# Three matmul passes per product against two: activation halves laid side by side in a two-block float32 kernel on one core

## The chip, the cores and the metric

The kernel runs on one core of one Trainium2 chip. The metric is device time in microseconds (us), the median of three runs. The engines named below are PE (TensorE, the matrix engine), DVE (VectorE), ACT (ScalarE), POOL (GpSimd) and SP (SyncE, which issues the weight DMAs). PE multiplies a moving operand (up to 512 columns) by 128x128 stationary weights and writes PSUM, a memory of eight banks of 512 float32 columns by 128 partitions.

## The reference

Two transformer blocks stand one behind the other, for 256 tokens of 1024 features, all in float32:

```
x = x + 0.5 * swiglu(rms_norm(x), gate 1024x2816, up, down 2816x1024)      # FFN1
h = rms_norm(x);  z = h @ w_in + b_in                                      # mix
x = x + (sig(g0) * (window_attention(z) @ w_a) + sig(g1) * (mlstm(z) @ w_m)) @ w_out
x = rms_norm(x + 0.5 * swiglu(rms_norm(x), ...))                           # FFN2
h = rms_norm_2(x);  z = h @ w_in                                           # mix2
x = x + concat(gated_linear_attention(z), latent_attention(z)) @ w_out
x = x + cross_attention(rms_norm_2(x), mem) @ w_o                          # xa
f = rms_norm_2(x)                                                          # FFN3
return x + (silu(causal_conv(f @ gate)) * (f @ up)) @ down
```

The result has to agree with this at float32 accuracy, so a single pass of reduced precision over a product is not enough.

## The kernel before

Activations lie mostly as [feature, token]: a tile of 128 features by T = 256 tokens, eight tiles for the 1024 features of `x`. Weights are streamed: SP fetches chunks of up to 1 MB into one of three raw buffers (`wraw`), and `halves` splits them into a high half `wh` (an ACT copy that rounds to the matrix format, L339) and a low half `wl` (a DVE subtraction, L340), six buffers each. Activations are split in the same way, `xh` by ACT and `xl` by DVE (`x_done`, L449 and L450, which also apply the norm's gain).

A float32 product is the sum of three passes, xh·wh + xl·wh + xh·wl. Where the result is wanted as [feature, token], `mm3` (L361 to L363) issues three matmuls of 256 moving columns for each 128x128 block of weights, all into the same 256 columns of PSUM. Where the result is wanted as [token, feature], `mm3n` (L367 to L369) has the weights moving, 272 to 512 columns; the diff leaves its three passes as they are. `mm3` is called 2208 times: 1584 in the three FFNs (each 44 column blocks by 8 for gate and up, 8 by 22 for down), 464 in mix, 160 in mix2 and xa.

`lin_t` computes a chunk of 256 output columns: two blocks j of 256 tokens, side by side in one PSUM bank. The PSUM pool `mm` has four buffers of one bank; the pool `at` has the four other banks. When a chunk is done, `scaled` (L512, L514) multiplies it by the norm's factor r per token on DVE, and so takes it out of PSUM. In an FFN a pair is one chunk of the gate (`pg`) and one of up (`pu`): s = pg·r, silu of it on ACT, a = s·pu, and the split of a. In FFN3 the gate passes a convolution over three tokens first (L562 to L564).

The instruction order on each engine comes from the framework's scheduler, which orders instructions by priorities and by its own estimate of when they can run; each engine then works strictly in that order and waits for semaphores of the others. A tile can be written again only when its last reader is through, so the number of PSUM buffers sets how far PE can run ahead of DVE and ACT.

Of the kernel before, what the change touches and what calls it, by code (L numbers as in the profile page):

```python
# [111 lines left out]
def column_vectors():  # L112
    """(key, input, index) of vectors by feature, 128 to a column."""
# [35 lines left out]
def lay_out(I):  # L149
    """The inputs as they lie in DRAM: the same numbers in another order."""  # L150
# [37 lines left out]
class Builder:  # L188
    """Activations lie as [feature, token] ("T") or as [token, feature] ("N"). A float32 product
    x*w is carried by three float32r passes over exact halves: xh*wh + xl*wh + xh*wl."""  # L190

    def __init__(self, ctx, tc, I, out):
# [6 lines left out]
        self.mm = pool("mm", 4, space=PSUM)  # L199
# [15 lines left out]
    def phase(self, name):  # L215
        """A pool for the tiles of one phase, also for its temporaries."""
# [9 lines left out]
    def pm(self):  # L226
        return self.mm.tile([P, 512], F32, tag="mm", name=self.n("mm"))
# [5 lines left out]
    def load_x(self):  # L233
        """x and the first weights, in the order of the features."""
# [20 lines left out]
    def row(self, name, a, n, tag, bufs=2):  # L255
        """Part of a row vector, on all partitions."""
# [5 lines left out]
    def consts(self):  # L262
# [19 lines left out]
        # gains of the latent attention's parts that aren't rotated, and the dimension's root  # L282
# [3 lines left out]
        # for the sums of squares of x * gain  # L286
# [4 lines left out]
        # additive masks of the window: [previous block | current block],  # L291
        # and of the causal attention: [all | current block]
# [7 lines left out]
        # [key, query] mask, once for each diagonal block of the mLSTM  # L300
# [9 lines left out]
        # minus the identity, once for each half  # L310
# [3 lines left out]
        # ones where source <= target  # L314
# [6 lines left out]
    def wraw(self, key, a=0, n=None):  # L321
        """A chunk (or elements a..a+n of each partition) of the weights."""
# [8 lines left out]
    def halves(self, v):  # L331
        """hi, lo of a view [P, n], n <= 1024."""
# [10 lines left out]
    def wcols(self, key, nt, kt=KD, per=1, early=False):  # L343
        """Halves of a "t" chunk as nt pairs [P, kt, 128]; per tiles of 128 columns are split at once."""
# [26 lines left out]
    def lin_t(self, key, xh, xl, kt=KD, early=False):  # L371
# [8 lines left out]
    def lin_n(self, key, n, xh, xl, kt=KD, pool=None):  # L380
        """Two PSUM tiles [128 tokens, n] of x @ (the "n" chunks of n columns), n <= 512."""
        ps = [(pool or self.pm)() for _ in range(TB)]
        for k, kk, runs in n_runs(n, kt):
            raw = self.wraw(f"{key}.{k}")
            for s, m in runs:
                hi, lo = self.halves(raw[:, s * n:(s + m) * n])
                for i in range(m):
                    q = k + s + i
                    for b in range(TB):
                        self.mm3n(ps[b][:, :n], xh[q][:, b * P:b * P + P], xl[q][:, b * P:b * P + P],  # L390
# [3 lines left out]
    def xtiles(self, k):  # L394
        xh = self.xp.tile([P, T], F32R, tag=f"xh{k}", name=self.n(f"xh{k}"))
        xl = self.xp.tile([P, T], F32R, tag=f"xl{k}", name=self.n(f"xl{k}"))
        return xh, xl

    def lin_first(self, key, xh, xl, raw=None):
        """Two PSUM views [P, 256] of x @ (a "t" chunk of 256 columns), that wait as little for the last of x.  # L400
        With raw, a "q" chunk, x too is split part by part."""
        ps = [self.pa()[:, :T] for _ in range(2)]
        if raw is None:
            hv = self.wcols(key, 2)
            for ks in (range(6), range(6, 8)):
                for j in range(2):
                    for k in ks:
                        self.mm3(ps[j], hv[j][0][:, k, :], hv[j][1][:, k, :], xh[k], xl[k], k == 0, k == 7)
        else:
            for q in range(4):  # L410
                for d in (2 * q, 2 * q + 1):
                    self.x_done(d)
                    xh.append(self.halved[d][0])
                    xl.append(self.halved[d][1])
# [8 lines left out]
    def rsqrt(self, y, v, shape):  # L423
        """y = 1/sqrt(v), by a step of Newton's method and one of third order."""
# [3 lines left out]
        # 3/8 of y * (3 - v y^2) / 2, then y * (15 - 10 h + 3 h^2) / 8, h = v y^2  # L428
# [11 lines left out]
    def then(self, gcol, tiles=None):  # L440
        """The gain of the norm that follows, and where the halves of x * gain go."""
        self.gcol, self.gtiles, self.halved = gcol, tiles or self.xtiles, {}

    def x_done(self, d):
        """Halves of x[d] * gain, for the norm that follows."""
        nc = self.nc
        h, l = self.gtiles(d)
        g = self.gcol[:, d:d + 1]
        nc.scalar.activation(h, self.x[d], AF.Copy, scale=g)  # L449
        nc.vector.scalar_tensor_tensor(l, self.x[d], g, h.bitcast(F32), ALU.mult, ALU.subtract)  # L450
        self.halved[d] = h, l

    def split_x(self):
        return [[self.halved[d][i] for d in range(KD)] for i in range(2)]
# [17 lines left out]
    def mean(self, acc, tag):  # L472
        """The mean over features by token, [P, TB]."""
# [6 lines left out]
    def sums(self, ps, i, acc):  # L480
        """Sums over partitions of acc[:, :T], to columns 2i, 2i+1 of ps."""
# [3 lines left out]
    def rinv_n(self, mean, tag="rN"):  # L485
        """1/rms by token, and the mean square with its guard."""
# [7 lines left out]
    def by_token(self, rn, tag="rB"):  # L494
        """[P, TB] (token on partitions) to [P, T], the same on all partitions."""
# [11 lines left out]
    def scaled(self, out, ps, r):  # L507
        """out [P, 2, T] = ps * r, ps being one PSUM tile or two."""
        tt = self.nc.vector.tensor_tensor
        if isinstance(ps, list):  # L510
            for j in range(2):
                tt(out[:, j, :], ps[j], r, ALU.mult)  # L512
        else:
# [1042 lines left out]
```

## Time and profile before

| | |
|---|---|
| median of 3 runs | 1031.64 us (1031.37 to 1032.19) |
| the profiled execution | known by its span, 1030.0 us from the first to the last instruction |
| PE busy | 1012.6 us, 98% of the span |
| DVE busy | 687.3 us, 67% |
| ACT busy | 548.7 us, 53% |
| POOL busy | 68.0 us, 7% |
| mean granted TensorE clock | 0.998 of full speed |

The span lies 1.64 us under the median: what stands around it (launch, end) is not in the trace. Busy time of PE is a modelled pipelined time, so that the distance from one matmul's start to the next says more on its pace than the duration in a row. "Idle before" in a row is the time in which an engine stood still ahead of these instructions, with what released it.

### The profile page before, as it was taken

What the parts mean: (1) busy time and instruction counts of PE and PEld (TensorE: products, weight loads), DVE (VectorE), ACT (ScalarE), POOL (GpSimd) and SP (SyncE); (2) the same over time, 40 slices, a digit from 0 to 9 for tenths busy, and PEclk for the clock granted to TensorE, in tenths of its full rate; (3) what the DMA queues carried; (4) which work ended last, traced back from release to release, by engine and by line L of the source; (5) the groups of instructions that cost most, each with busy time, mean ns of one, the idle gap of its engine ahead of it and who ended that gap; (6) DMA issues with size and microseconds to landing.
All of it is one profiled execution on the core that took longest, in us unless ns stands there. A gap on an engine that the chain in (4) does not pass through costs nothing.

```text
span 1030.0 us, 18987 instructions
## 1 busy us (share of the span) xinstructions
PE 1012.6 (98%) x7770; PEld 964.4 (94%) x7770; DVE 687.3 (67%) x1212; ACT 548.7 (53%) x936; POOL 68.0 (7%) x200
## 2 busy tenths in 40 slices
PE   6999999999999999999999999999899999999998
PEld 6999999999866799999999999998789899999998
DVE  7756556557966657567655665678967778777642
ACT  5644444458745554545544544468855656655431
POOL 4200000010000010000100020012000401000000
PEclk9999999999999999999999999999999999999999
DMA  6755545545343325445554645446305425555560
GB/s 229 268 183 186 179 169 185 185 167 207 128 155 129 123 92 196 164 164 197 188 190 173 226 160 182 160 163 221 148 2 205 164 87 210 195 175 183 161 199 22
DMA packets 28520, 173.00 MB, mean 168 GB/s; under 512 B 3712, under 2 KB 5008, under 8 KB 10128
## 3 DMA queue, kind: packets, MB, share of 16 engines
q1 hardware_dynamic: 26640, 169.88, 46.7%
q10 hardware_dynamic: 1728, 1.88, 0.6%
q8 instruction: 61, 1.00, 0.4%
q14 instruction: 27, 0.22, 0.1%
q0 software_dynamic: 64, 0.02, 0.0%
HBM read 170.72 MB, written 1.05 MB: 167 GB/s over the span
## 4 chain that ended last, share of the span: by engine, by line
PE 93%; DVE 2%; DMA 2%; POOL 1%; issue 1%; ACT 0%; DVEq 0%; POOLq 0%; ACTq 0%
PE mm L362 24%; PE mm L363 24%; PE mm L361 24%; PE mm L367 3%; PE mm L368 3%; PE mm L369 3%; PE at L656 1%; PE at L692 1%; DMA wr<-in_wts 1%; PE at L363 1%; PE at L362 1%; PE at L361 1%; DVE wl L340 1%; PE at L687 1%; DMA posi<-in_pos 1%
## 5 line engine op out<-in xcount | busy, mean ns | idle before, releaser
L339 ACT ACTIVATE wh<-wr 128x1024 fp32r<-128x1024 f32 (+5 forms) x380 | 340.3, 913 | 375.2 <-PE mm L362 262.1
L340 DVE TENSOR_TENSOR wl<-wr,wh 128x1024 fp32r<-128x1024 f32 (+5 forms) x380 | 391.8, 1043 | 209.8 <-ACT wh L339 208.7
L363 PE MATMUL mm<-xh,wl 128*128 128x256 f32 x1296 | 367.2, 283 | 0.2 <-DVE wl L340 0.2
L362 PE MATMUL mm<-xl,wh 128*128 128x256 f32 x1296 | 367.3, 283 | 0.0
L361 PE MATMUL mm<-xh,wh 128*128 128x256 f32 x1296 | 367.2, 284 | 0.0
L363 PEld LDWEIGHTS mm<-xh,wl 128*128 128x128 f32 x1296 | 248.6, 192 | 0.7 <-DVE wl L340 0.4
L362 PEld LDWEIGHTS mm<-xl,wh 128*128 128x128 f32 x1296 | 248.6, 192 | 0.3 <-issue 0.3
L361 PEld LDWEIGHTS mm<-xh,wh 128*128 128x128 f32 x1296 | 248.5, 192 | 0.1
L361 PE MATMUL mm<-ah,wh 128*128 128x256 f32 x528 | 149.5, 283 | 0.0
L362 PE MATMUL mm<-al,wh 128*128 128x256 f32 x528 | 149.4, 283 | 0.0
L363 PE MATMUL mm<-ah,wl 128*128 128x256 f32 x528 | 149.4, 283 | 0.0
L362 PEld LDWEIGHTS mm<-al,wh 128*128 128x128 f32 x528 | 101.4, 192 | 0.0
L361 PEld LDWEIGHTS mm<-ah,wh 128*128 128x128 f32 x528 | 101.4, 192 | 0.0
L363 PEld LDWEIGHTS mm<-ah,wl 128*128 128x128 f32 x528 | 101.4, 192 | 0.0
L367 PE MATMUL mm<-wh,xh 128*128 128x512 f32 (+2 forms) x160 | 61.6, 386 | 0.0
L369 PE MATMUL mm<-wh,xl 128*128 128x512 f32 (+2 forms) x160 | 61.2, 382 | 0.0
L368 PE MATMUL mm<-wl,xh 128*128 128x512 f32 (+2 forms) x160 | 60.7, 380 | 0.0
L367 PEld LDWEIGHTS mm<-wh,xh 128*128 128x128 f32 x160 | 30.1, 188 | 7.1 <-issue 2.3
L363 PE MATMUL mm<-b16h,wl 128*128 128x256 f32 x128 | 36.3, 284 | 0.0
L362 PE MATMUL mm<-b16l,wh 128*128 128x256 f32 x128 | 36.2, 283 | 0.0
L361 PE MATMUL mm<-b16h,wh 128*128 128x256 f32 x128 | 36.2, 283 | 0.0
L368 PEld LDWEIGHTS mm<-wl,xh 128*128 128x128 f32 x160 | 30.1, 188 | 5.8 <-issue 1.1
(510 smaller groups left out, 1341.9 us busy)
## 6 DMA issues: line engine op xcount, KB each, us to landing
wr<-in_wts SPq DMA_DIRECT2D x141, 1024.0 KB, 4.8
wr<-in_wts SPq DMA_DIRECT2D x12, 768.0 KB, 4.3
wr<-in_wts SPq DMA_DIRECT2D x6, 512.0 KB, 4.4
wr<-in_memt SPq DMA_DIRECT2D x2, 1024.0 KB, 5.6
wr<-in_wts SPq DMA_DIRECT2D x2, 864.0 KB, 4.4
wr<-in_wts SPq DMA_DIRECT2D x6, 256.0 KB, 5.1
bb<-in_rows ACTq DMA_DIRECT2D x6, 256.0 KB, 3.5
wr<-in_wts SPq DMA_DIRECT2D x2, 544.0 KB, 4.0
```

Of the source, the lines that this page charges most:

```text
L339: nc.scalar.activation(hi[:, i:i + m], v[:, i:i + m], AF.Copy)
L340: nc.vector.tensor_tensor(lo[:, i:i + m], v[:, i:i + m], hi[:, i:i + m].bitcast(F32), ALU.subtract)
L361: mm(ps, wh, xh, start=start, stop=False)
L362: mm(ps, wh, xl, start=False, stop=False)
L363: mm(ps, wl, xh, start=False, stop=stop)
L367: mm(ps, xh, wh, start=start, stop=False)
L368: mm(ps, xh, wl, start=False, stop=False)
L369: mm(ps, xl, wh, start=False, stop=stop)
L656: nc.tensor.matmul(ps[:, i * nk:i * nk + nk], aq[p][g * per + i][hs, b * P:b * P + P], ak[p][hs, 0:nk], start=True, stop=True)
L687: nc.tensor.transpose(pt[:, j * P:j * P + P], S[:, j, kb * P:kb * P + P], self.ident)
L692: nc.tensor.matmul(po[hs, :], av[:, kb, kv * 64:kv * 64 + 64], pTs[kb], start=kb == 0, stop=kb == b)
```

## The change

The two halves of an activation tile are put into one tile `xs` [128, 2, 256], high half first. `mm3` then issues two matmuls: `wh` by all 512 columns of `xs` into a full bank, and `wl` by the high half (256 columns) into the bank's second half. The first half of the bank then holds xh·wh and the second xl·wh + xh·wl; they are added when the bank is evacuated (`joined`: an ACT copy of the second half, a DVE addition of the first, and, where a factor r is due, a DVE multiplication in SBUF). A chunk of `lin_t` now takes two banks, and the pool `mm` has two buffers of two banks. Where an evacuation used to be one addition to `x` (xo, wo), it is now two additions.

```diff
-        self.mm = pool("mm", 4, space=PSUM)
+        self.mm = pool("mm", 2, space=PSUM)
...
-        return self.mm.tile([P, 512], F32, tag="mm", name=self.n("mm"))
+        return self.mm.tile([P, 2, 512], F32, tag="mm", name=self.n("mm"))
...
-    def mm3(self, ps, wh, wl, xh, xl, start, stop):
+    def mm3(self, ps, wh, wl, xs, start, stop):
         mm = self.nc.tensor.matmul
-        mm(ps, wh, xh, start=start, stop=False)
-        mm(ps, wh, xl, start=False, stop=False)
-        mm(ps, wl, xh, start=False, stop=stop)
+        mm(ps, wh, xs, start=start, stop=False)
+        mm(ps[:, T:], wl, xs[:, 0, :], start=False, stop=stop)
...
-                self.mm3(ps[:, j * T:j * T + T], hv[j][0][:, k, :], hv[j][1][:, k, :], xh[k], xl[k], k == 0, k == kt - 1)
+                self.mm3(ps[:, j, :], hv[j][0][:, k, :], hv[j][1][:, k, :], xs[k], k == 0, k == kt - 1)
...
-    def scaled(self, out, ps, r):
...
+    def joined(self, ps, out=None, r=None):
+        nc = self.nc
+        if out is None:
+            out = self.tmp([P, 512], "z").rearrange("p (j t) -> p j t", j=2)
+        for p, o in [(ps[j], out[:, j, :]) for j in range(2)] if isinstance(ps, list) else [(ps, out)]:
+            nc.scalar.activation(o, p[..., T:], AF.Copy)
+            nc.vector.tensor_tensor(o, p[..., :T], o, ALU.add)
+        if r is not None:
+            nc.vector.tensor_tensor(out, out, self.bc2(r), ALU.mult)
+        return out
...
-                    self.scaled(J(s), pg, r)
+                    self.joined(pg, J(s), r)
...
-                nc.vector.tensor_tensor(a, s, pu, ALU.mult)
+                self.joined(pu, J(a))
+                nc.vector.tensor_tensor(a, s, a, ALU.mult)
...
-                    y = ft([P, T], "dy", 2)
-                    nc.vector.tensor_tensor(y, ps[j][:, :T], rh, ALU.mult)
-                    nc.vector.tensor_tensor(x[d], x[d], y, ALU.add)
+                y = self.joined(ps, J(ft([P, 512], "dy", 2)), rh)
+                nc.vector.tensor_tensor(J(self.x2[dp]), J(self.x2[dp]), y, ALU.add)
...
-                nc.vector.tensor_tensor(z[:, :, 3:], J(ps), self.bc2(rB), ALU.mult)
+                self.joined(ps, z[:, :, 3:], rB)
```

Two places show how this moves instructions. The first is PE's order at the end of pm (the last projection before the output projection wo; its last chunk is `mm_749` before and `mm_715` after). Before, three chunks of wo (`mm_756`, `mm_766`, `mm_776`) are begun on the feature tiles that are ready:

```order
L363 MATMUL mm_749_4995<-b16h_679_4492,wl_748_4992 128x256
L361 MATMUL mm_756_5062<-sg_721_4782,wh_752_5054 128x256 [waits Activation_49]
L362 MATMUL mm_756_5062<-v1_722_4783,wh_752_5054 128x256 [waits DVE_49]
...
L361 MATMUL mm_776_5200<-sg_721_4782,wh_772_5192 128x256
L362 MATMUL mm_756_5062<-v1_722_4783,wh_752_5054 128x256 [waits DVE_49]
L363 MATMUL mm_756_5062<-sg_721_4782,wl_753_5055 128x256
```

After, there are two such chunks (`mm_722`, `mm_730`), and the second of them waits for the buffer:

```order
L369 MATMUL mm_715_4137<-b16_647_3740,wl_714_4134 128x256
L368 MATMUL mm_722_4188<-vs_688_3973,wh_718_4180 128x512 [waits DVE_49]
L369 MATMUL mm_722_4188<-vs_688_3973,wl_719_4181 128x256
...
L368 MATMUL mm_730_4239<-vs_688_3973,wh_726_4231 128x512 [waits DVE_49]
L369 MATMUL mm_730_4239<-vs_688_3973,wl_727_4232 128x256
...
L369 MATMUL mm_730_4239<-vs_688_3973,wl_727_4232 128x256
L368 MATMUL mm_722_4188<-vs_688_3973,wh_718_4180 128x512 [waits DVE_49]
```

What moved: the filling work between the end of pm and the feature tiles that come from its last chunk went from parts of three chunks (48 matmuls) to parts of two (24 matmuls).

The second is DVE's order from the output projection of the cross attention (`x0` to `x3` are pairs of tiles of x) to FFN3's activations. Before, one addition for each tile (L1498, L1504) stands ahead of the first low half `xl0`:

```order
L1498 TENSOR_TENSOR x0_85<-mm_1483_9443,x0_85 128x256 [waits PE_49]
L1498 TENSOR_TENSOR x0_85<-mm_1484_9444,x0_85 128x256 [waits PE_49]
L1498 TENSOR_TENSOR x1_88<-mm_1485_9445,x1_88 128x256 [waits PE_49]
L1498 TENSOR_TENSOR x1_88<-mm_1486_9446,x1_88 128x256 [waits PE_49]
L340 TENSOR_TENSOR wl_1538_9715<-wr_1536_9712,wh_1537_9714 128x512 [waits DMAHW4_49,Activation_49]
L1504 TENSOR_TENSOR x2_91<-at_1510_9557,x2_91 128x256 [waits PE_49]
L340 TENSOR_TENSOR wl_1538_9715<-wr_1536_9712,wh_1537_9714 128x512 [waits Activation_49]
L1504 TENSOR_TENSOR x2_91<-at_1511_9558,x2_91 128x256 [waits PE_49]
L450 SCALAR_TENSOR_TENSOR xl0_1498_9525<-x0_85,cols_82,xh0_1497_9524 128x256 [waits Activation_49]
```

After, two additions for each tile (L1476, L1483), ten of them ahead of `xs0`:

```order
L1476 TENSOR_TENSOR x0_85<-mm_1388_7849,x0_85 128x256 [waits PE_49]
...
L1476 TENSOR_TENSOR x1_88<-mm_1389_7850,x1_88 128x256 [waits PE_49]
L1483 TENSOR_TENSOR x2_91<-at_1407_7943,x2_91 128x256 [waits PE_49]
L346 TENSOR_TENSOR wl_1430_8068<-wr_1428_8065,wh_1429_8067 128x512 [waits Activation_49]
L1483 TENSOR_TENSOR x2_91<-at_1408_7944,x2_91 128x256 [waits PE_49]
L1476 TENSOR_TENSOR x0_85<-mm_1388_7849,x0_85 128x256 [waits DVE_49]
L346 TENSOR_TENSOR wl_1432_8074<-wr_1428_8065,wh_1431_8073 128x512 [waits Activation_49]
L1483 TENSOR_TENSOR x3_94<-at_1409_7945,x3_94 128x256 [waits PE_49]
L346 TENSOR_TENSOR wl_1432_8074<-wr_1428_8065,wh_1431_8073 128x512 [waits Activation_49]
L1476 TENSOR_TENSOR x1_88<-mm_1389_7850,x1_88 128x256 [waits DVE_49]
L1476 TENSOR_TENSOR x1_88<-mm_1389_7850,x1_88 128x256
L467 SCALAR_TENSOR_TENSOR xs0_1398_7911<-x0_85,cols_82,xs0_1398_7911 128x256 [waits Activation_49]
```

What moved: from the first addition to `x0` up to FFN3's first activation tile DVE now has ten additions and four low halves of weights, where it had six and two.

## Rows read from the trace of the kernel before

**Rows 1.** The page: busy times, and the chain that ended last.
```profile
PE 1012.6 (98%) x7770; PEld 964.4 (94%) x7770; DVE 687.3 (67%) x1212; ACT 548.7 (53%) x936; POOL 68.0 (7%) x200
...
PE 93%; DVE 2%; DMA 2%; POOL 1%; issue 1%; ACT 0%; DVEq 0%; POOLq 0%; ACTq 0%
PE mm L362 24%; PE mm L363 24%; PE mm L361 24%; PE mm L367 3%; PE mm L368 3%; PE mm L369 3%; PE at L656 1%; PE at L692 1%; DMA wr<-in_wts 1%; PE at L363 1%; PE at L362 1%; PE at L361 1%; DVE wl L340 1%; PE at L687 1%; DMA posi<-in_pos 1%
```

**Rows 2.** Waits of PE: line, releaser, total us, times, longest us.
```profile
PE at L1157 <- DVE qT L1145: 3.2, 1, 3.2
```

**Rows 3.** Windows: stretch, length, busy us (instructions) by engine, clock, DMA share, GB/s.
```profile
30.00:40.00 10.00, 9.47 (x80) 9.27 (x79) 8.46 (x10) 5.50 (x7) 6.35 (x10) 1.00 0.94 340
...
270.00:280.00 10.00, 10.00 (x60) 8.71 (x59) 9.96 (x27) 9.60 (x23) 0.00 (x0) 1.00 0.55 191
...
730.00:740.00 10.00, 6.85 (x38) 5.80 (x37) 9.69 (x32) 8.74 (x33) 1.43 (x7) 0.88 0.40 148
```

**Rows 4.** Groups by line on PE: busy us, mean ns of one, idle before.
```profile
L362 PE MATMUL mm<-xl,wh 128*128 128x256 f32 x1296 | 367.3, 283 | 0.0
...
L361 PE MATMUL mm<-ah,wh 128*128 128x256 f32 x528 | 149.5, 283 | 0.0
```

**Rows 5.** Timeline of PE in FFN1: start us, duration; first and last of 26.
```profile
99.95 0.28 PE L362 MATMUL mm<-xl,wh 128*128 128x256 f32 x1
...
102.95 0.28 PE L363 MATMUL mm<-xh,wl 128*128 128x256 f32 x1
```

**Rows 6.** Timeline of PE in xa, 512 columns; first and last of 14.
```profile
802.06 0.39 PE L368 MATMUL mm<-wl,xh 128*128 128x512 f32 x1
...
805.03 0.39 PE L369 MATMUL mm<-wh,xl 128*128 128x512 f32 x1
```

**Rows 7.** Groups by line on DVE, 860 to 960 us (FFN3's gate and up).
```profile
L340 DVE TENSOR_TENSOR wl<-wr,wh 128x1024 fp32r<-128x1024 f32 x35 | 42.9, 1224 | 14.1 <-ACT wh L339 13.8
L563 DVE SCALAR_TENSOR_TENSOR s<-g,cols,s 128x256 f32<-128x256 f32 x22 | 9.6, 478 | 0.0
...
L514 DVE TENSOR_TENSOR g<-mm,rB 128x512 f32<-128x512 f32 x10 | 6.9, 689 | 4.4 <-PE mm L363 4.3
```

**Rows 8.** Groups by line on ACT, 860 to 960 us.
```profile
L339 ACT ACTIVATE wh<-wr 128x1024 fp32r<-128x1024 f32 x34 | 36.0, 1060 | 38.3 <-PE mm L362 26.4 <-issue 7.8 <-ACT s L562 4.1
...
L572 ACT ACTIVATE ah<-a 128x512 fp32r<-128x512 f32 x10 | 6.2, 618 | 0.0
```

**Rows 9.** The chain's pieces at the start: start us, us, what.
```profile
35.74 1.21 POOL rN L438
37.03 0.69 PE at L499 x4
```

**Rows 10.** Timeline of xa, one head's softmax: sums, row maximum, scaled probabilities.
```profile
811.59 0.50 PE L483 MATMUL at<-ones,usq 128*128 128x1 f32 x4
...
816.51 0.16 DVE L1432 SCALAR_TENSOR_TENSOR m<-m,rq 128x2 f32<-128x2 f32 x1 [0.34 <-POOL rq L438]
...
819.51 0.61 DVE L1440 TENSOR_SCALAR S<-S,l 128x256 f32<-128x256 f32 x2
```

**Rows 11.** Groups by line on DVE, 830 to 850 us (xa's end, FFN3's start).
```profile
L340 DVE TENSOR_TENSOR wl<-wr,wh 128x512 fp32r<-128x512 f32 x12 | 7.8, 684 | 2.0 <-ACT wh L339 2.0
L450 DVE SCALAR_TENSOR_TENSOR xl<-x,cols,xh 128x256 fp32r<-128x256 f32 x8 | 3.5, 479 | 0.0
...
L1498 DVE TENSOR_TENSOR x<-mm,x 128x256 f32<-128x256 f32 x4 | 1.4, 417 | 2.8 <-PE mm L363 2.8
```

**Rows 12.** Timeline of the end.
```profile
1025.82 0.28 PE L363 MATMUL mm<-ah,wl 128*128 128x256 f32 x1
1026.14 0.42 DVE L590 TENSOR_TENSOR dy<-mm,rh 128x256 f32<-128x256 f32 x1 [1.27 <-PE mm L363]
1026.60 0.42 DVE L591 TENSOR_TENSOR x<-x,dy 128x256 f32<-128x256 f32 x1
```

**Rows 13.** Windows of 1 us on PE after its longest idle time.
```profile
738.00:739.00 1.00, 1.00 (x5) 0.50 0.66 213
```

More of the change, by code (lines that the diff above doesn't have):

```diff
@@ L226, in pm, with banks @@
     def pm(self):
-        return self.mm.tile([P, 512], F32, tag="mm", name=self.n("mm"))
+        return self.mm.tile([P, 2, 512], F32, tag="mm", name=self.n("mm"))
+    def banks(self):
+        return [t[:, j, :] for t in (self.pm(), self.pm()) for j in range(2)]
     def pa(self):
@@ L394, in xtiles, with lin_first @@
     def xtiles(self, k):
[L395 to L402, printed above, removed]
+        return self.xp.tile([P, 2, T], F32R, tag=f"xs{k}", name=self.n(f"xs{k}"))
+    def lin_first(self, key, xs, raw=None):
+        ps = [self.pa() for _ in range(2)]
         if raw is None:
@@ L446, in x_done, with split @@
         nc = self.nc
[L447 to L451, printed above, removed]
-    def split_x(self):
-        return [[self.halved[d][i] for d in range(KD)] for i in range(2)]
+        s = self.gtiles(d)
+        self.split(s, self.x[d], self.gcol[:, d:d + 1])
+        self.halved[d] = s
+    def split_x(self):
+        return [self.halved[d] for d in range(KD)]
+    def split(self, s, v, gain=None):
+        nc = self.nc
+        h, l = s[:, 0], s[:, 1]
+        if gain is None:
+            nc.scalar.activation(h, v, AF.Copy)
+            nc.vector.tensor_tensor(l, v, h.bitcast(F32), ALU.subtract)
+        else:
+            nc.scalar.activation(h, v, AF.Copy, scale=gain)
+            nc.vector.scalar_tensor_tensor(l, v, gain, h.bitcast(F32), ALU.mult, ALU.subtract)
     def squares(self, x2, pool=False):
@@ L505, in bc2 @@
         return t[:, None, :].to_broadcast([P, 2, T])
-    def scaled(self, out, ps, r):
[L509 to L513, printed above, removed]
-            tt(out, ps.rearrange("p (j t) -> p j t", j=2), self.bc2(r), ALU.mult)
+    def joined(self, ps, out=None, r=None):
+        nc = self.nc
+        if out is None:
[6 more added lines that the diff above has]
+        return out
     def ffn(self, f, half, nxt=None, conv=False, last=False, first=False, mem=False):
@@ L529, in products @@
                 if pr == 0:
-                    pg = self.lin_first(f"{f}g{pr}", xh, xl, self.first if first else None)
+                    pg = self.lin_first(f"{f}g{pr}", xs, self.first if first else None)
                 else:
-                    pg = self.lin_t(f"{f}g{pr}", xh, xl)
-                pairs[pr] = pg, self.lin_t(f"{f}u{pr}", xh, xl, early=first and pr == 0)
+                    pg = self.lin_t(f"{f}g{pr}", xs)
+                pairs[pr] = pg, self.lin_t(f"{f}u{pr}", xs, early=first and pr == 0)
             if not first:
@@ L557, in ffn @@
                     nc.vector.memset(g[:, :, 0:2], 0.0)
-                    self.scaled(g[:, :, 2:], pg, r)
+                    self.joined(pg, g[:, :, 2:], r)
                     for j in range(2):
@@ L874, in mix @@
                 for j in range(2):
[L875 to L883 removed]
+                    nc.vector.scalar_tensor_tensor(ym[:, j, :], g1[2 * dp + j], 1.0, ym[:, j, :], ALU.add, ALU.mult)
@@ L884, in mix @@
+                nc.vector.tensor_tensor(ym, ym, ya[:, 2 * dp:2 * dp + 2, :], ALU.add)
+                self.split(gs[:, :, 2 * dp:2 * dp + 2, :], ym)
             self.then(self.col("gff2", 0, 8))
             for dp in range(4):
-                ps = self.lin_t(f"wo{dp}", mh, ml)
+                ps = self.lin_t(f"wo{dp}", [gs[:, :, k, :] for k in range(8)])
+                xd = J(self.x2[dp])
+                for i in range(2):
+                    nc.vector.scalar_tensor_tensor(xd, ps[:, :, i * T:i * T + T], 0.5, xd, ALU.mult, ALU.add)
@@ L984, in mix2 @@
             with self.phase("mix2") as mp:
-                mem = self.mix2_heads(mp, ot, xh, xl, mh, ml)
+                mem = self.mix2_heads(mp, ot, xs, ms)
             with self.phase("xa") as mp:
-                self.then(self.col("gxa", 0, 8), lambda d: [mp.tile([P, T], F32R, tag=f"x{s}{d}", name=self.n("xm")) for s in "hl"])
+                self.then(self.col("gxa", 0, 8), lambda d: mp.tile([P, 2, T], F32R, tag=f"xs{d}", name=self.n("xm")))
                 for c in range(2):
                     hv = self.wcols(f"wo2{2 * c}", 2) + self.wcols(f"wo2{2 * c + 1}", 2)
-                    ps = [(self.pm, self.pa)[c]() for _ in range(4)]
+                    ps = self.banks() if c == 0 else [self.pa() for _ in range(4)]
                     ks = ((4, 5, 6, 7), (0, 1, 2, 3))[::1 - 2 * c]
@@ L1029, in mix2_heads @@
                 nc.tensor.transpose(pt[:, b * P:b * P + P], cz[:, b, i * P:i * P + P], self.ident)
-            hl = mt([P, 2, T], f"st{i}", dt=F32R)
-            h_, l_ = hl[:, 0, :], hl[:, 1, :]
-            nc.scalar.activation(h_, pt[:, :T], AF.Copy, scale=gains[i])
-            V.scalar_tensor_tensor(l_, pt[:, :T], gains[i], h_.bitcast(F32), ALU.mult, ALU.subtract)
-            ch.append(h_)
-            cl.append(l_)
+            cs_.append(mt([P, 2, T], f"st{i}", dt=F32R))
+            self.split(cs_[-1], pt[:, :T], gains[i])
         sc = mt([P, 3, TB], "sc")
@@ L1234, in mix2_heads @@
         nc.scalar.activation(keN.rearrange("p b f -> p (b f)"), pt, AF.Copy)
-        pts = [self.pm(), self.pm()]
+        pts = self.pm()
+        pts = [pts[:, r, :] for r in range(2)]
         for c in range(2):
@@ L1292, in mix2_heads @@
         grs = mt([P, TB, 4], "grs")
-        po = []
+        po = self.pm()
+        po = [po[:, b, :] for b in range(TB)]
         for b in range(TB):
-            pt = self.pm()
+            pt = po[b]
             for j in range(2):
@@ L1344, in xa_memory @@
         g = self.col("gmem", 0, 8)
[L1345 removed]
+        ts = []
         for d in range(KD):
[L1347 to L1353 removed]
+            ts.append(self.xtiles(d))
+            self.split(ts[d], raw[:, d * T:d * T + T], g[:, d:d + 1])
+        return ts
     def xa_norm(self):
@@ L1487, in xa @@
         hv = self.wcols("xo0", 4, 4, per=2)
-        ps = [self.pm() for _ in range(4)]
+        ps = self.banks()
         out(ps, hv, [(0, j) for j in range(4)])
@@ L1497, in xa @@
         for j in range(4):
-            V.tensor_tensor(x[j], ps[j][:, :T], x[j], ALU.add)
+            for i in range(2):
+                V.tensor_tensor(x[j], ps[j][:, i * T:i * T + T], x[j], ALU.add)
             self.x_done(j)
@@ L1503, in xa @@
         for j in range(4):
-            V.tensor_tensor(x[4 + j], ps[j][:, :T], x[4 + j], ALU.add)
+            for i in range(2):
+                V.tensor_tensor(x[4 + j], ps[j][:, i * T:i * T + T], x[4 + j], ALU.add)
             self.x_done(4 + j)
```

219 lines of the change are left out of this document (86 added, 133 removed).

## The prediction

> **What bounds the kernel now.** I read the busy table first, then the chain, the waits of PE, and the stretches of 10 us. PE is busy 1012.6 us of 1030.0, and 93% of the chain that ended last is PE, 72% of it the three passes of `mm3` alone [rows 1]. The other engines have room on average (DVE 67%, ACT 53%), but not everywhere: from 270 to 280 us DVE works 9.96 us of 10 while PE still is full, and at 730 us PE has its one long wait behind DVE, 3.2 us [rows 2, 3]. So a saving on PE is a saving in time wherever DVE and ACT can follow, and every stage must be looked at for whether they can.
>
> **What is saved.** The duration of a matmul in its group (283 ns, [rows 4]) is not its cost, because matmuls overlap; the cost is the distance between starts. In FFN1, 25 intervals of 256-column matmuls take 102.95 − 99.95 = 3.00 us, 0.120 us each [rows 5]. In xa, 13 intervals of 512-column matmuls take 805.03 − 802.06 = 2.97 us, 0.2285 us each [rows 6]. Three passes of 256 columns cost 0.360 us; one of 512 and one of 256 cost 0.2285 + 0.120 = 0.3485. The columns are the same 768; what goes is one fixed part per matmul, 2 × 0.120 − 0.2285 = 11.5 ns. With 2208 products: 2208 × 11.5 ns = 25.4 us. The new 512-column matmul moves activations instead of weights, but of the same type and width as that in the rows, so I take the rows' price. The bounds: nothing, if the pair keeps the pace of three (then each product costs 0.360 as before), and 29 us, if the 256-column matmul behind the wide one came at the pure column rate (1.7 ns less each by (0.2285 − 0.120)/256 = 0.424 ns per column, 0.3468 us).
>
> The Trainium skill's page "TensorE: Matmul & The Clock Gate", section "Back-to-back issue gap", gives a distance of N/2.4 + 2.5 ns at full clock. By it a wide matmul would replace two narrow ones for a gain of 2.5 ns, 2208 × 2.5 ns = 5.5 us in all, an estimate from that page. The rows show a fixed part four to five times as large (0.120 us against 256/2.4 = 0.107), and I go by the rows.
>
> **What is added on DVE and ACT in the steady stages.** Each evacuation of a chunk gains an ACT copy of 512 columns, 0.62 us [rows 8], and a DVE operation of 512 columns, 0.69 [rows 7]. In an FFN3 pair DVE has now four low halves (4 × 1.22), four convolution steps (4 × 0.478) and three operations of 512 columns (3 × 0.69): 8.9 us of the pair's 32 × 0.360 = 11.5. After, two additions more: 10.3 of 32 × 0.3485 = 11.15. That still fits, at 92%. FFN1 and FFN2 have no convolution: 4 × 1.22 + 3 × 0.69 = 7.0 becomes 8.3. The buffers: a gate chunk has 5.6 us (the up chunk's PE time) before its buffer is wanted again. Its evacuation is a copy of 0.62, an addition of 0.69 and what DVE has in hand, a low half of 1.22 and perhaps the copy ahead of that on ACT (1.06, [rows 8]): 3.1 to 3.6 us. So two buffers are enough in steady stages and I put the loss there at 0; without this cover each microsecond per pair costs 11 in FFN3.
>
> **What is lost at the transitions.** Here PE waits for the last of one stage before the next, and the longer evacuation is on the path. One by one:
>
> 1. Start. By-token factors of FFN1 wait for POOL, which ends rN at 36.95, and PE starts at 37.03 [rows 9]; that chain does not get shorter with PE. The 64 products ahead of it (64 × 11.5 ns = 0.74) gain nothing, and an addition of 0.69 now stands ahead of the chain's DVE step: −1.5 (0 to −2).
> 2. Mix, 240 to 285 us. Four `mqk` chunks bring 4 × 0.69 = 2.8 us more to a DVE that is full from 270 to 280 [rows 3], though their factor has to be applied as before. I take −2.0 (0 to −5: hidden behind PE's full buffers, or all of it and two other chunks' as well).
> 3. pm to wo. After mm_715's end its buffer comes free after some 2.85 us (copy 0.62, the rest of a low half of 1.22, the addition 0.69 and the hand-overs); PE has four products, 1.4 us: −1.45. Then come eight more products, 2.8 us, beside a chain of 3.5 us (a low half of 512 columns, two steps of 256, an addition, a copy, a low half): −0.75. Together −2.2 (0 to −4).
> 4. mix2, with two buffers in turn: −0.7 (0 to −2).
> 5. xa. One head's softmax goes from its sums to its scaled probabilities in 820.1 − 811.6 = 8.5 us [rows 10], most of it POOL and DVE steps, which the change leaves alone. The queries and values that PE does meanwhile are now shorter, and the value product is used up earlier: −2.0 (0 to −4).
> 6. xa to FFN3. After the output projection's first half PE has 11 products left, 3.8 us. DVE's row to the first activation tile holds ten additions at about 0.36 (four took 1.4 us together with their overlap), four low halves of 512 columns at 0.62 to 0.68 and the split at 0.48, about 7.0 us [rows 11]; before it was six and two, 4 us. PE waits some 3.1 us for the first tile, and 2.9 for the second, which has four low halves and three additions ahead of it: −6.0 (−2 to −9). It does no other work then, so the clock may fall too: after the idle time at 733 us the granted clock was 0.50, 1.2 GHz, at 738 [rows 13], and the stretch of 10 us had a mean of 0.88 [rows 3]. That is in the lower end.
> 7. End. The last product's DVE steps are 0.42 + 0.42 now [rows 12]; after, a copy of 0.62 and three steps of 0.69 for two tiles at once, 2.7 us: −1.8 (−1.5 to −2.2).
>
> The other transitions (FFN1 to mix, wo to FFN2, FFN2 to mix2, wo2 to xa) have 7 to 9 us of PE work beside chains of 3 to 5.5 us: 0, and some 2 each if a chain queues behind three low halves.
>
> The losses sum to 1.5 + 2.0 + 2.2 + 0.7 + 2.0 + 6.0 + 1.8 = 16.2. The net is −25.4 + 16.2 = −9.2 us, from a span of 1030.0 to 1020.8. The median stands 1.64 above the span, and I add as much: 1022.4, rounded to 1022.
>
> **Rivals.**
>
> Nearly the full gain. If the waits at 2 to 6 are absorbed (DVE catches up, because half of its time is free on either side), only start and end remain: 1031.6 − 25.4 + 3.3 = 1009.5. For it speaks that PE today stands still for only 17 us (1030.0 − 1012.6, [rows 1]) in spite of such chains; against it, that in 6 the order on DVE leaves it no room.
>
> Slower, because DVE's strict order waits for ACT. The new addition cannot start before ACT's copy, and ACT may be in a weights copy of 1.06 us. Then DVE stands still with low halves behind it, and the wl buffers run dry in FFN3's gate and up. A pair has 0.85 us of room. With two such waits of up to 1.06 + 0.62 = 1.7 us DVE needs 10.3 + 3.4 = 13.7 us for a pair, and 11 pairs lose 11 × 2.5 = 28 us. It decides from 10.3 + 1.7 = 12.0 us per pair on, where the 9.2 of the forecast are gone. I price it at half-way, waits of 1.1 us each: 12.5 us, 11 × 1.35 = 15 us, 1037. For it speaks that DVE today waits 13.8 of 100 us there for that very copy [rows 7]; against it, that DVE has other rows between the matmul's end and the addition.
>
> No gain per product. If two narrow matmuls' fixed part remains beside a wide one (the pace set by something other than the number of matmuls), only losses remain: 1031.6 + 16.2 = 1047.8. Rows 6 speak against it, since they show wide matmuls in sequence at 0.2285; only the alternation of wide and narrow is not shown. A smaller fixed part is a case of the same kind: if only a fifth of the 11.5 ns were saved, 5 us, the time would be 1031.6 − 5.1 + 16.2 = 1042.7. The rule of the Trainium skill cited above would put it there, too, at 1042.3 as an estimate from it.
>
> **How the numbers follow.** The forecast has 0.64, the nearly full gain 0.18, the wait for ACT 0.11, and no gain or a small one per product 0.07 (0.03 and 0.04). What a measurement of this kernel tells from no change is 0.2%, 2.1 us: faster means under 1029.6. The first two cases are faster (0.82); the wait for ACT lies in its mild half about no change (0.06) and in its hard half above (0.05), and no gain per product is slower: 0.12 slower. The forecast's own range is 1016 to 1029, by those ends of its terms that do not all meet. Down to the full gain and up to the mild half of the wait for ACT it is 1009 to 1033; 0.04 lie below, 0.13 above.
>
> **What would show it.** In FFN1 starts of a wide and a narrow matmul alternate at 0.2285 and 0.120 us, and a pair takes 11.15. If they lie at 0.24 and 0.12, the saving is wrong from the ground. PE's waits should list the first tiles of FFN3 with some 3 us each, and a few waits of 1 to 2 us behind evacuations in mix, at wo and in xa; DVE should be busy about 92% in FFN3's pairs, without waits of PE there. Waits of PE in each pair of FFN3 for low halves, with DVE idle behind an ACT copy, would bring the slow rival. The end should be about 1.8 us longer from the last matmul's start. If the waits in xa and at FFN3 are missing, the result is nearer to 1010.

## The result, and the profile after

The change makes the kernel slower: 1043.95 us, median of 4 runs from 1039.12 to 1049.71, against 1031.51 (1031.06 to 1032.19). The ratio is 1.0125, 95% interval 1.0086 to 1.0164. The forecast was 1022, range 1009 to 1033: wrong in sign. The traced execution took 1041.34 us, with a span of 1039.6. Of the runs below, one execution of e2 (1129.48 us, at a mean granted clock of 0.841) is a slow one and is left out of e2's median.

The page of the changed kernel, answering to [rows 1]: busy times, and the chain that ended last.

```profile
PE 998.3 (96%) x5562; PEld 848.6 (82%) x5562; DVE 753.4 (72%) x1309; ACT 598.8 (58%) x1041; POOL 66.1 (6%) x200
...
PE 88%; DVE 4%; DMA 2%; ACT 2%; POOL 1%; issue 1%; ACTq 0%; DVEq 0%
```

PE works 14.3 us less, yet the span is 9.6 longer: PE's idle time went from 17.4 to 41.3 us. DVE has 66 us more work and ACT 50. The waits of PE of the changed kernel (total us, times, longest us) name the places:

```profile
PE at L368 <- DVE xs L467: 8.4, 2, 7.3
PE mm L368 <- DVE z L527: 6.1, 2, 4.6
PE mm L368 <- DVE xs L467: 3.4, 1, 3.4
PE at L1147 <- ACT g2k L1353: 3.0, 1, 3.0
PE at L1428 <- DVE S L1421: 2.3, 1, 2.3
PE mm L373 <- ACT wh L345: 2.0, 1, 2.0
PE at L1308 <- DVE czog L1302: 1.9, 2, 1.6
...
PE mm L368 <- DVE a L527: 1.3, 1, 1.3
```

The 7.3 us stand at the start of the program (7.0 before), the 3.0 in mix2 (3.2 before, [rows 2]). The others shown are new. The pace itself is about as forecast. In FFN3 of the changed kernel 29 products lie between these two starts, 10.05 us, 0.3466 us each ([rows 5, 6] gave 0.3485):

```profile
989.83 0.39 PE L368 MATMUL mm<-ahl,wh 128*128 128x512 f32 x1
...
999.88 0.39 PE L368 MATMUL mm<-ahl,wh 128*128 128x512 f32 x1
```

The clock adds to the waits. Windows of the changed kernel (length, busy us by engine, granted clock behind POOL's), at the begin of mix and at FFN3's start:

```profile
226.00:228.00 2.00, 0.00 (x0) 0.00 (x0) 0.89 (x2) 1.68 (x5) 0.00 (x0) 1.00 0.51 139
...
230.00:232.00 2.00, 2.00 (x7) 1.67 (x7) 1.03 (x2) 1.54 (x4) 0.00 (x0) 0.50 0.00 0
...
840.00:845.00 5.00, 2.60 (x6) 1.55 (x6) 5.00 (x15) 2.86 (x6) 0.00 (x0) 0.59 0.53 185
845.00:850.00 5.00, 3.93 (x12) 3.36 (x13) 5.00 (x14) 2.72 (x6) 0.00 (x0) 0.50 0.64 234
850.00:855.00 5.00, 5.00 (x28) 4.35 (x27) 1.71 (x3) 0.57 (x2) 0.00 (x0) 0.89 0.01 3
```

After the waits of 4.58, 2.99 and 3.39 us (mix, mix2, FFN3) PE goes on at half clock, 1.2 GHz, in mix and mix2 for some 3 us, at FFN3 for some 10. The kernel before has one such stretch, of some 3 us in mix2. The Trainium skill's page "TensorE: Matmul & The Clock Gate", section "Part 1: The HAM clock gate (the "warmup" mystery)", says that an idle engine is throttled to half and that sustained work releases it; these rows agree.

### The profile page after: what moved, and what is told of

Its sections match the earlier page's. It is cut to its first block, busy times and chain, and to the rows that moved or that the text cites. A ratio compares the mean times of both kernels' runs of the same rounds, so it can differ in the third digit from the quotient of the medians.

```text
span 1039.6 us, 14827 instructions
## 1 busy us (share of the span) xinstructions
PE 998.3 (96%) x5562; PEld 848.6 (82%) x5562; DVE 753.4 (72%) x1309; ACT 598.8 (58%) x1041; POOL 66.1 (6%) x200
## 4 chain that ended last, share of the span: by engine, by line
PE 88%; DVE 4%; DMA 2%; ACT 2%; POOL 1%; issue 1%; ACTq 0%; DVEq 0%
PE mm L368 44%; PE mm L369 22%; PE mm L373 3%; PE mm L375 3%; PE mm L374 3%; DVE wl L346 2%; PE at L368 2%; DMA wr<-in_wts 1%; PE at L666 1%; PE at L702 1%; PE at L369 1%; ACT wh L345 1%; PE at L697 1%; DMA x<-in_xt 1%; PE at L807 0%
## 5 line engine op out<-in xcount | busy, mean ns | idle before, releaser
L368 PE MATMUL mm<-xs,wh 128*128 128x512 f32 x1296 | 459.5, 399 | 9.2 <-DVE z L527 4.6
L369 PE MATMUL mm<-xs,wl 128*128 128x256 f32 x1296 | 364.2, 281 | 0.2 <-DVE wl L346 0.2
L368 PEld LDWEIGHTS mm<-xs,wh 128*128 128x128 f32 x1296 | 244.6, 189 | 67.7 <-issue 10.8
L369 PEld LDWEIGHTS mm<-xs,wl 128*128 128x128 f32 x1296 | 246.2, 190 | 0.9 <-DVE wl L346 0.6
L368 PE MATMUL mm<-ahl,wh 128*128 128x512 f32 x528 | 184.3, 395 | 0.0
L369 PE MATMUL mm<-ahl,wl 128*128 128x256 f32 x528 | 147.7, 280 | 0.0
L368 PEld LDWEIGHTS mm<-ahl,wh 128*128 128x128 f32 x528 | 99.0, 188 | 23.0
L369 PEld LDWEIGHTS mm<-ahl,wl 128*128 128x128 f32 x528 | 99.7, 189 | 0.0
L373 PE MATMUL mm<-wh,xs 128*128 128x512 f32 (+2 forms) x160 | 60.9, 381 | 2.0 <-ACT wh L345 2.0
L375 PE MATMUL mm<-wh,xs 128*128 128x512 f32 (+2 forms) x160 | 60.9, 381 | 0.0
L374 PE MATMUL mm<-wl,xs 128*128 128x512 f32 (+2 forms) x160 | 60.8, 380 | 0.0
```

The source lines that it names most:

```text
L368: mm(ps, wh, xs, start=start, stop=False)
L369: mm(ps[:, T:], wl, xs[:, 0, :], start=False, stop=stop)
L373: mm(ps, xh, wh, start=start, stop=False)
L374: mm(ps, xh, wl, start=False, stop=False)
L375: mm(ps, xl, wh, start=False, stop=stop)
```

## Where the time went, stage by stage

The traces have the same landmarks (last product of an FFN, factors by token, transposes). From their times I take how much longer each stage took than before, in the one traced execution of each kernel. The kernels other than the changed one are those of the next section.

| stage, longer than before by (us) | changed | e3 evacuation | e5 narrow | e11 xa narrow | e8 FFNs only |
|---|---|---|---|---|---|
| start to FFN1's last product | −3.6 | +0.5 | +0.4 | −7.0 | −5.6 |
| to the end of pm (mix) | +2.2 | −0.4 | +4.5 | +1.8 | 0.0 |
| to the end of wo | +3.2 | 0.0 | +2.9 | +3.2 | 0.0 |
| to FFN2's last product | −7.9 | 0.0 | −1.4 | −7.9 | −3.7 |
| to the last transposes of mix2 | +2.2 | +1.2 | +4.7 | +3.7 | 0.0 |
| to the last values of xa | +8.7 | 0.0 | +3.7 | +4.0 | 0.0 |
| to the end of xo | −1.1 | +0.1 | +0.2 | −1.0 | +0.1 |
| to FFN3's factors by token | +8.1 | +5.2 | +6.6 | +1.9 | −0.3 |
| to FFN3's last product | −4.7 | 0.0 | +0.7 | −4.6 | −3.3 |
| to the end of the span | +2.4 | +2.0 | +2.5 | +2.4 | +0.9 |

The FFNs give about what was forecast (16.2 us, their own waits included, of 18.2). Nearly everything between them, and the end, takes it back with interest. The trace of e11 is of its fastest execution (1028.11 us, median 1034.09), and so is that of e8 (1019.64, median 1022.77); their columns are more favourable than their medians.

## The experiments

**e3: the longer evacuation alone.** The kernel before, four buffers and narrow matmuls, with evacuations of the change's length.

```diff
+            nc.scalar.activation(o, p, AF.Copy)
+            nc.vector.tensor_tensor(o, p, o, ALU.max)
...
-                    nc.vector.scalar_tensor_tensor(x[d], ps[:, j * T:j * T + T], 0.5, x[d], ALU.mult, ALU.add)
+                for i in range(2):
+                    nc.vector.scalar_tensor_tensor(self.x2[dp], ps, 0.25, self.x2[dp], ALU.mult, ALU.add)
```

> The kernel before, with four buffers and three narrow matmuls, but evacuations as long as those of the change: an ACT copy and a DVE maximum of bank and copy ahead of each multiplication, two additions of a part instead of one for wo and xo (the result is the same). Not copied: wo2 and the queries of xa. Theory (both together): 1036 to 1046 us, with waits at the end of xa as in the changed kernel. Rival (the longer evacuation alone makes the losses): 1058 us or more. Rival (the few buffers alone): 1031.5 us.

Measured: 1040.22 us, ratio 1.0084 (1.0069 to 1.0099), within the theory's interval. In its trace 5.2 us are at FFN3's start, 2.0 at the end, 1.2 in mix2, 0.5 in FFN1; mix, wo and the other FFNs hide it. PE's idle times at FFN3's start in e3, after the last products of xo:

```profile
839.33 0.38 PE L361 MATMUL at<-xh,wh 128*128 128x256 f32 x1 [2.56 <-DVE x L1518]
840.33 0.39 PE L362 MATMUL at<-xl,wh 128*128 128x256 f32 x1 [0.61 <-DVE xl L450]
```

So the doubled additions ahead of the first activation tile are a loss by themselves, where the prediction put it. But all that e3 shows is 8.6 us, about a third of what e5 (below) loses with the same PE work.

**e2: two PSUM buffers alone.** The kernel before with the change's PSUM pool.

```diff
-        self.mm = pool("mm", 4, space=PSUM)
+        self.mm = pool("mm", 2, space=PSUM)
...
+        t = self.mm.tile([P, 2, 512], F32, tag="mm", name=self.n("mm"))
+        return [t[:, j, :] for j in range(2)]
```

> The kernel before with only its PSUM pool changed: two buffers of two banks instead of four of one bank, a chunk using the first bank of its buffer, evacuations as before. Theory (losses come from the longer evacuation and from the few buffers together): 1033 to 1042 us. Rival (the few buffers alone make the losses of some 35 us): 1058 us or more. Rival (the longer evacuation alone makes them): 1031.5 us.

Measured: 1074.5 us, ratio 1.042 (1.0398 to 1.0442): far outside my theory's interval and inside that of the first rival. PE waits for `r L442`, `s`, `g` and `aq`: a chunk that leaves PSUM by its multiplication with r must wait for r, and with two buffers PE stands before r is there. At the last products of FFN1 and FFN2 e2 is 9.4 and 23.5 us behind the kernel before, where the changed kernel is 3.6 and 6.1 ahead. So this run overstates the buffers' part in the change, whose copy and addition need no r; the next one is fitter for it.

**e5: everything of the change but the wide matmul.**

```diff
-        mm(ps, wh, xs, start=start, stop=False)
+        if start:
+            mm(ps, wh, xs, start=True, stop=False)
+        else:
+            mm(ps[:, :T], wh, xs[:, 0, :], start=False, stop=False)
+            mm(ps[:, T:], wh, xs[:, 1, :], start=False, stop=False)
         mm(ps[:, T:], wl, xs[:, 0, :], start=False, stop=stop)
```

> The changed kernel with its layout, buffers and evacuations, but narrow matmuls: only the first product of each bank is a wide and a narrow one, all others (some 1950 of 2208) are three of 256 columns. Theory (the wide matmul saves 6.6 to 13 ns per product, as its trace shows, and the losses lie elsewhere): 1950 times 11.7 ns are 23 us, so about 1044 + 23 = 1067 us, 1058 to 1070 since some waits are then covered by longer PE work. Rival (a wide and a narrow matmul together save nothing on PE): 1044 us.

Measured: 1055.12 us, ratio 1.0225 (1.0208 to 1.0242). The page of e5:

```profile
span 1054.8 us, 18757 instructions
...
PE 1019.7 (97%) x7532; PEld 958.1 (91%) x7532; DVE 753.4 (71%) x1309; ACT 599.2 (57%) x1041; POOL 68.1 (6%) x200
```

The wide matmul is worth 11.2 us in time (1055.1 − 1043.95), less than half of the 23 expected, and PE's busy time differs by 21.4. The time lies below the theory's interval and above the rival's value. By the stages the FFNs gain 4.0 + 6.5 + 5.4 = 15.9 us, more than the 15.2 between the two spans; the mixers together gain nothing (mix 2.3 and mix2 2.5 better, xa 5.0 worse). The saving is on PE, but in the mixers PE only comes earlier to something that is late.

Together with e3 this splits the change, in medians: evacuations +8.7, two buffers beside them +14.9 (1055.1 − 1040.2), the wide matmul −11.2. The sum is +12.4. The middle term is a remainder: it holds all that e5 has and e3 has not, the evacuations of wo2 and of xa's queries among it. Nor do the parts add up in any order, since the two buffers cost 43 us beside the short evacuation (e2).

**e6: the first mixer's wait.** In the changed kernel PE stands still at the begin of mix, ACT and DVE do this (start us, us, what):

```profile
224.83 0.38 ACT L514 ACTIVATE rB<-at 128x256 f32<-128x256 f32 x1
...
225.60 1.29 DVE L529 TENSOR_TENSOR z<-z,rB 128x512 f32<-128x512 f32 x2
...
226.32 1.70 ACT L631 ACTIVATE aq<-z,cols 128x256 f32<-128x256 f32 x4 [1.11 <-DVE z L529]
227.93 1.05 ACT L526 ACTIVATE z<-mm 128x512 f32<-128x512 f32 x2
228.54 1.29 DVE L527 TENSOR_TENSOR z<-mm,z 128x512 f32<-128x512 f32 x2 [1.65 <-ACT z L526]
```

Both `z` buffers hold joined chunks that wait for the factor rB. Only when they are multiplied and read can the next two chunks be copied out of PSUM, and then PE goes on at 229.38, after 4.58 us. e6 joins into the final tiles instead:

```diff
-                z = self.joined(ps, r=rB)
...
+                    nc.scalar.activation(t, p[:, T:], AF.Copy)
+                    nc.vector.tensor_tensor(t, p[:, :T], t, ALU.add)
```

> The changed kernel, but the first mixer's queries and keys are joined straight into their own tiles, two of 256 columns, without the z buffers. Theory (at FFN1 to mix PE waits 4.6 us because both z buffers hold chunks that wait for the factor by token, so that no third chunk can leave PSUM; and it then runs at half clock for 3 to 4 us): that wait is gone, 5 to 8 us less, about 1037 us. Rival (the wait comes from the number of PSUM buffers or from DVE's work): no change, 1044 us.

Measured: 1037.29 us (1034.57 to 1041.85), ratio 1.0067 (1.0044 to 1.009), 6.7 less than the changed kernel and where the theory put it. The trace shows the `z` wait of 4.6 us gone and with it the half clock behind it, another wait of 2.2 us in its place, and 3.6 us less from FFN1's end to the end of pm:

```profile
PE mm L368 <- DVE aq L632: 2.2, 1, 2.2
```

So the mechanism is shown, at about half of its price; the rest of the 6.7 is within the spread of the two kernels.

**e7 and e11: xa, narrow.** e7 takes the wide matmul and the second addition from the output projection of xa; e11 also from the queries and from mix2's output projection.

```diff
-                self.mm3(ps[j], hv[j][0][:, k, :], hv[j][1][:, k, :], os_[k], k == 0, k == 3)
+                self.mm3c(ps[j][:, :T], hv[j][0][:, k, :], hv[j][1][:, k, :], os_[k], k == 0, k == 3)
...
-            for i in range(2):
-                V.tensor_tensor(x[j], ps[j][:, i * T:i * T + T], x[j], ALU.add)
+            V.tensor_tensor(x[j], ps[j][:, :T], x[j], ALU.add)
```

> The changed kernel, but the output projection of the cross attention has three narrow matmuls into 256 columns and one addition for each tile, as before the change. Theory (the doubled additions on DVE make PE wait for FFN3's first tiles and then run at half clock): the two waits of 3.4 and 1.1 us shrink to under 1 and the half clock goes, 5 to 9 us less, 1035 to 1039 us. Rival (it is the fewer PSUM buffers, or the order): 1043 us or more.

> The changed kernel with three narrow matmuls and single evacuations in the output projection of mix2, in the queries and in the output projection of xa; the PSUM pool stays two buffers of two banks. The first trace lost 8.7 us from the end of mix2's heads to the last values of xa, and 8.1 from there to FFN3. Theory (in xa it is the two PSUM buffers, at FFN3 the doubled additions): xa's loss stays at 6 to 9 us, FFN3's goes to some 3; 1037 to 1041 us. Rival (in xa, too, it is the longer evacuation): both go, about 1031 to 1034 us.

Measured: e7 1040.73 us (1034.56 to 1043.16), ratio 1.0078, between the theory and its rival; e11 1034.09 (1028.11 to 1039.61, 10 runs), ratio 1.0026 (1.001 to 1.0043). In e7 the stage from xo to FFN3's factors goes from +8.1 to +3.4, as expected, but xa before it from +8.7 to +12.2: half a gain. The loss in xa need not be the edit's: in e7's trace the clock fell to half three times from 764 to 826 us (mean 0.89), in the changed kernel's once. In e11 the stage goes to +1.9, and xa to +4.0. FFN3's start in e11 has one wait left:

```profile
834.12 0.50 PE L368 MATMUL at<-xs,wh 128*128 128x512 f32 x1 [2.26 <-DVE xs L473]
```

e11's time fell where the rival put it, yet the rival's reason does not hold: e5, with all long evacuations of xa and narrow matmuls, also loses only 3.7 in xa, and e2, with the evacuations of before, 3.3. So of xa's 8.7 us some 3.5 go with the two buffers. In e2 and e11 most of that is order: 20 matmuls (2.4 us at 0.120) stand inside the stage that stood outside it before. About 5 come only with the wide matmuls. The stage as a window, before and then in the changed kernel:

```profile
769.73:826.83 57.10, 56.44 (x398) 52.23 (x397) 42.99 (x93) 32.56 (x75) 11.49 (x44) 1.00 0.47 166
```

```profile
766.12:831.60 65.48, 59.69 (x317) 50.38 (x317) 47.76 (x107) 33.00 (x75) 9.65 (x44) 0.98 0.41 145
```

PE stands still 5.8 us there (0.7 before, 1.4 in e11), 2.3 of them for the softmax chain of [rows 10] and 2.0 for weights, and some 3 us at half clock cost 1.5 (clock 0.66 from 765 to 770 us). For the weights ACT itself waits for the DMA:

```profile
789.84 2.19 ACT L345 ACTIVATE wh<-wr 128x512 fp32r<-128x512 f32 x4 [1.99 <-DMA wr<-in_wts]
```

No run separates these two waits from the wide matmuls' other order of instructions.

**e10: the same kernel again.**

> The changed kernel once more, unchanged, for a second trace. In the first, a wide and a narrow matmul took 0.3534 us in FFN1 and 0.3466 in FFN2 and FFN3. Theory A (the pace belongs to the program, by its addresses or its code): the same stages have the same paces again. Theory B (it differs from execution to execution, which would also explain why the changed kernel's times spread over 10 us where those of before spread over 1 to 2): other stages are slow this time.

Measured: one run, 1043.05 us. FFN1 again has 0.353 us for a product, but FFN3, 0.3466 in the first trace, now has 10.24 / 29 = 0.3531:

```profile
989.64 0.40 PE L368 MATMUL mm<-ahl,wh 128*128 128x512 f32 x1
...
999.88 0.40 PE L368 MATMUL mm<-ahl,wh 128*128 128x512 f32 x1
```

Theory B holds for FFN3. The waits of 4.58 us at mix and 3.39 at FFN3 stand in this trace again, to the hundredth, so they are not a chance of one execution.

**e8 and e9: the change in the FFNs alone.** Four buffers of one bank, each block joined from its own bank, the mixers as before; in e9 also FFN3's last two blocks narrow.

```diff
-                    pg = self.lin_t(f"{f}g{pr}", xh, xl)
+                    pg = self.lin_w(f"{f}g{pr}", xs)
...
+    def lin_w(self, key, xs, kt=KD, early=False):
+        hv = self.wcols(key, 2, kt, early=early)
+        ps = [self.pm() for _ in range(2)]
```

> The kernel before with the change in the three FFNs alone: there a wide and a narrow matmul per product into a bank of its own, joined bank by bank; four PSUM buffers of one bank; mix, mix2 and xa as before. Theory (the saving is real, the losses belong to the mixers and to the end): 528 times 6.6 ns and 1056 times 13.3 ns are 17.5 us, less 0.5 at the start and 2.4 at the end and about 1 in FFN3: 1018 us, 1014 to 1022. Rival (the longer evacuation binds FFN3, where DVE then works 10.6 us of a pair's 11.1): 1026 us or more.

> As the kernel with the change in the FFNs alone, but the last two column blocks of FFN3's down projection are again three narrow matmuls into 256 columns, taken out by one multiplication. Theory (the end after the last matmul lengthened by the joined evacuation, some 2 us): 1020.5 us, 1018 to 1023, and the last matmul's start to the end of the span as before the change (4.2 us). Rival (the output's DMA hides it): 1022.8 us.

Measured: e8 1022.77 us (1019.64 to 1027.8), ratio 0.9921 (0.989 to 0.9952), 0.8 above the theory's interval and under the rival's; e9 1022.35 (1020.23 to 1026.02), ratio 0.9913 (0.9896 to 0.993). The page of e8:

```profile
span 1017.9 us, 16193 instructions
...
PE 996.2 (98%) x6186; PEld 875.9 (86%) x6186; DVE 737.9 (72%) x1365; ACT 589.9 (58%) x1092; POOL 70.1 (7%) x200
```

PE is back at 98%, and the 12.1 us come out of the FFNs one after the other. The joined evacuation does not bind FFN3's pairs, even with 256-column pieces: PE has no wait there. But FFN3 and its start give only 3.6 us of the 7.0 of their pace, since PE now waits 2.9 us for FFN3's factors:

```profile
PE at L542 <- POOL rN L481: 2.9, 1, 2.9
```

In e9 the end (last product to the end of the span) is 4.2 us, as before, against 5.1 in e8; in the medians 0.4 is not told from nothing, so theory and rival stay open. These two are the fastest kernels of the study.

**e12: the mixer kept wide, but mended** (the edits of e6 and e11, and a narrow end).

> The changed kernel with three mends: queries and keys of the first mixer joined straight into their tiles, the output projection of mix2 and all of xa narrow with single evacuations, and FFN3's last column blocks narrow. The wide form remains in the FFNs and the first mixer, with two PSUM buffers of two banks. Theory (the mixers' losses come from waits that the few buffers make, so their wide matmuls are worth little): 1034.1 less 3.6 (the first mixer, as its trace showed) less 1 (end): 1029.5 us, 1026 to 1032, above the kernel with the FFNs alone changed (1022.5). Rival (the mixers' wide matmuls pay once the waits are mended): 1020 us or less.

Measured: 1027.96 us (1026.31 to 1032.62), ratio 0.9953 (0.9935 to 0.9971). Faster than before and within the theory's interval, slower than e8 and e9, though its interval touches e8's. By the stages of its trace mix and wo lose 3.8 us, in e8 nothing: the first mixer's 464 wide products do not pay for the two buffers.

## Why the prediction was wrong

- The saving per product was about right: 0.3466 to 0.3533 us against 0.3485, that is 6.7 to 13.4 ns against 11.5, and 15.9 us in the FFNs by e5. So the rival of a small saving, 5.5 us in all by the rule that the prediction cites, did not come. The prediction's upper bound of 29 us does not follow from its own figures: at 0.424 ns per column a matmul of 256 columns takes 0.1085 us, 11.5 ns less and not 1.7, which would bound the saving at 51 us.
- The steady stages were right: a single wait of 1.3 us in FFN3's pairs, DVE busy 88% there (forecast 92%), so the rival of DVE waiting for ACT did not come.
- The step that failed is "The losses sum to 16.2". In the trace PE stands still 23.9 us longer than before and loses some 8.5 us more to the half clock (half the length of each such stretch), 32.4 in all. As the span grew by 9.6, the saving was by this count 22.8, near the 25.4 of the forecast. By term, in us:

| term | forecast loss | standing still | half clock |
|---|---|---|---|
| 1, start | 1.5 | 0.0 | 0 |
| 2 and FFN1 to mix | 2.0 + 0 | 4.6 | 1.7 |
| 3, pm to wo | 2.2 | 1.9 | 0 |
| 4, mix2 | 0.7 | 4.2 | 0.2 |
| 5, xa | 2.0 | 5.1 | 1.5 |
| 6, FFN3's start | 6.0 | 4.5 | 5.1 |
| FFN3's pairs | 0 | 1.3 | 0 |
| 7, end | 1.8 | 2.4 | 0 |

These are windows of the two traces between the landmarks of the stages. Those of FFN1 to pm, mix2 and FFN3's start (length, PE's busy time first, the granted clock behind POOL's), before:

```profile
204.47:451.70 247.23, 247.23 (x1709) 217.85 (x1708) 169.28 (x356) 139.64 (x283) 7.83 (x22) 1.00 0.44 154
665.90:769.73 103.83, 100.66 (x630) 87.41 (x629) 81.75 (x222) 75.86 (x199) 16.36 (x60) 0.98 0.37 132
834.89:858.80 23.91, 23.91 (x203) 23.91 (x201) 17.73 (x32) 13.45 (x23) 4.03 (x11) 1.00 0.59 213
```

And in the changed kernel:

```profile
200.86:450.35 249.49, 244.91 (x1307) 198.21 (x1306) 182.05 (x377) 150.62 (x306) 7.32 (x23) 0.99 0.43 153
659.77:766.12 106.35, 98.97 (x577) 83.41 (x577) 82.82 (x223) 77.30 (x203) 16.86 (x60) 0.98 0.37 129
838.68:870.69 32.01, 27.49 (x137) 22.98 (x136) 23.78 (x47) 16.30 (x29) 3.90 (x11) 0.84 0.45 157
```

- The sentence "the other transitions ...: 0" missed FFN1 to mix. I had compared PE's cover of 7 to 9 us with a chain of 3 to 5.5 us, and not asked how many chunks may be out of PSUM before the factor rB is there. Two PSUM buffers and two `z` buffers made it 4.6 us and half clock; e6 shows that mechanism for 3.6 us of it.
- Term 6, FFN3's start: the waits of 3.4 and 1.1 us were forecast as 3.1 and 2.9, but the half clock, which I kept for the range's end, was there for 10 us. That doubled additions make this loss is shown by e3 (5.2 us with four buffers) and by e7 and e11, which take it back.
- Term 5, xa: the forecast's mechanism, a chain that does not get shorter, is there (the softmax wait of 2.3 us), but it is one part. The two buffers, the wait for the weights' DMA and the clock were not in the term.
- Term 4, mix2, was 0.7 and measured 4.4. New there are waits of 1.3 us for kT, 1.6 for czog and shorter ones. By the stages e3 loses 1.2, e5 4.7 and e2 10.4, so that the longer evacuation alone does not make it; how the two buffers do was not looked into.
- Term 3, pm to wo, was right in its wait: 1.9 us against 2.2. The stage grew by 3.2, since besides this wait four products of FFN2 (1.4 us) now run in it. Neither part of the change makes the wait alone: the stage grows by 0.0 in e3 (long evacuation, four buffers) and by 0.0 in e2 (two buffers, short evacuation), by 2.9 in e5, which has both.
- Terms 1 and 2 were too dark: FFN1's factors come 0.5 us earlier than before, and mix as a whole loses 2.2 us, less than the wait and the half clock at its start.
- The rival "slower" had the right sign by a mechanism that did not come, with a chance of 0.11. Of the range it can be said that 7 items of one sign, each with an open lower end, do not fail independently: most hang on two buffers, on the longer evacuation or on the one clock.

## What to carry to other kernels

Count, for a change that frees the bound engine by loading PSUM and the evacuating engines, every place where the bound engine waits for the end of a stage; the steady stages tell little. Ask at each how many results can be parked before a late factor arrives, over all pools on the way, not in PSUM alone. Apply such a change only where a steady stage pays for it: here the two passes are worth −0.8 to −0.9% in the FFNs alone, with four buffers of one bank, and +1.25% everywhere, with two of two.

## What the hardware showed that was not expected

A product of a wide and a narrow matmul has two paces, about 0.3466 and 0.3533 us, at a granted clock of 1.00. An FFN mostly has the one or the other throughout, and which may change from execution to execution (FFN3 in the two traces of the changed kernel; in e8 FFN1 has 0.3466 and FFN2 0.3533; in e6 and e7 FFN2 has 0.3533 in gate and up and 0.3466 in down). Three narrow matmuls had 0.360 in every FFN looked at. Over 2208 products the difference is 15 us, enough for the 10.6 us by which the changed kernel's runs differ, where those before differ by 1 to 3. That it makes this spread is not shown: the mean granted clock differs too, 0.984 in the slowest run and 0.990 in the fastest, though in e11's ten runs (0.991 to 0.996) it does not follow the time. Why the pace differs stays open; no run here looked for the cause.

Whether a shorter wait is followed by half clock also changes from execution to execution. In the changed kernel's first trace the clock fell after a wait of 1.64 us at the end of mix2 and not after one of 2.26 us in xa; in its second trace it was the other way round (1.67 us without, 2.28 us with half clock). In e11 and e12 the same wait of 2.3 us at FFN3's start was followed by full clock in the one and by half clock in the other.
